# Row sums of attention: who reads the total out of its bank, and where the two rows are added

## The chip, the core and the metric

The kernel runs on one core of one Trainium2 chip. The core has TensorE (PE, matmuls; PEld is its weight load), VectorE (DVE), ScalarE (ACT), GpSimd (POOL) and SyncE (SP), whose queue issues the transfers. The engines run side by side, each in the order of its own instructions, and wait for each other on semaphores. The metric is the device time of one execution in microseconds; lower is better.

## What is computed

A decoder layer on 2048 tokens of width 1024: one input projection, causal attention with 8 heads on one side, a gated unit on the other, one output projection and a layer norm. The change touches the attention alone:

```
def one_block(args):
    qi, i = args
    sc = jnp.einsum('bqhd,bkhd->bhqk', qi, k).astype(jnp.float32) * scale
    ...
    sc = jnp.where(mask[None, None], sc, -jnp.inf)
    p = jax.nn.softmax(sc, axis=-1).astype(v.dtype)
    return jnp.einsum('bhqk,bkhd->bqhd', p, v)
```

The softmax divides by the sum of the exponentials of a query. The kernel sums them unnormalized and multiplies with the reciprocal at the end, together with the gate z_a.

## The kernel before

Three stages follow each other: projections and the gated unit (up to some 530 us), attention (to some 1010 us, with the first blocks of the output projection mixed in), and the rest of the output projection with the layer norm.

Attention works head by head (h = 0 to 7) and, in a head, by query tiles of 512 queries (qt = 0 to 3). Scores are laid out with keys on partitions and queries along the free axis. A unit is one block of 128 keys against one query tile: three matmuls of scores (L425 to L427, a high and a low part of each operand), the exponential on ACT in place in the bank (L435, `bank_a`), a high part by a cast on ACT (L441, `ph` or `xbuf`), the low part on DVE (L101, `pl`), and two matmuls with the values some four units later (L469 and L470, `bank_b`). POOL adds up the high parts over a tile's units (L454 and L456, `acc`), which is the larger part of the row sums. Meanwhile PE, DVE and ACT make the maxima of the next head's scores (L352 on PE into `bank_c`, L362 and L359 on DVE) and its keys and values. `bank_c` has two buffers, which these jobs and the total below share.

At the end of a tile, `finish_ops` folds the results. ACT copies half of one bank to `opair` (L527) and the whole other bank, which holds the low parts' sums and outputs, to `bsb` (L531); DVE and POOL add (L534, L537). For qt > 0, ACT casts `acc` to a high part (L555, `acch`), POOL makes the remainder (L101, `accl`), and PE multiplies both with ones (L564, `total`), so that every partition of a `bank_c` bank holds the total of the row sums. DVE adds one partition of this total to the row in `bsb` (L567, `row`), and SP gathers the row of 512 numbers onto 128 partitions by 4 (L581, `lc`). DVE takes the reciprocal there (L586), SP stores it to memory (L587, `r_d`), and for the odd head of a pair loads it back, spread over the partitions (L599, `rb`, two loads). POOL multiplies `opair` with the gate and with `rb` (L603), and SP stores the product (L609, `oa_d`). For qt = 0 there is no total and the row of `bsb` is gathered as it is.

The order on the engines is not that of the code. Every step is an `Op` with an engine, a cost from `LENGTH` (a fixed part and one per element), a rank and its dependences; `issue()` then picks, time step by time step in this model, the ready op of lowest rank, with buffers limited by `COUNT`. A different engine or cost for one op therefore moves other work on all engines. Each engine waits in its own order: an instruction that waits holds all behind it on that engine, transfers on SP's queue included. Loads of the last stage, such as those of `ln_g` into a buffer of `opair` (L1530), are placed on SP's queue among the last heads' transfers.

Of the kernel before, what the change touches and what calls it, by code (L numbers as in the profile page):

```python
# [15 lines left out]
ALU = mybir.AluOpType  # L16
# [40 lines left out]
def hybrid_layer_kernel(ctx: ExitStack, tc: tile.TileContext, xT, x, pos, w_feat, w_v, w_c,  # L57
# [3 lines left out]
    act, dve, pool, pe, sp = nc.scalar, nc.vector, nc.gpsimd, nc.tensor, nc.sync  # L61
# [35 lines left out]
    def f(ap):  # L97
        return ap.bitcast(F32)

    def sub(eng, out_, a, b):  # L100
        eng.tensor_tensor(out=out_, in0=a, in1=b, op=ALU.subtract)  # L101
# [7 lines left out]
    def bank_c():  # L109
        return ps_c.tile([P, 512], F32, name="bank_c")  # L110
# [40 lines left out]
    def raw2k(shape):  # L151
        return sb.tile(shape, F32, name="raw", tag="raw", bufs=5)
# [21 lines left out]
    def t2_tile(shape, dt, name, bufs):  # L174
        return pools["t2"].tile(shape, dt, name=name, tag=name, bufs=bufs)
# [94 lines left out]
    def op(eng, n, rank, fn, deps=(), times=1, takes=(), pair=None):  # L270
        fixed, per = LENGTH[eng]
        o = Op(eng, times * (fixed + per * n), rank, fn, deps, LAG[eng])
        o.takes += takes
        o.pair = eng == "pool" and n > 0 if pair is None else pair
        work.append(o)
        return o
# [128 lines left out]
    def tile_ops(h, qt, t_, q_, k_, e, g, own, oth):  # L405
# [5 lines left out]
        for n, j in enumerate(order):  # L411
# [99 lines left out]
            units.append(un)  # L511
            done["s"][h, qt] = s_
        finish_ops(h, qt, t_, e, own, oth, units[-1]["pv"], len(units) - 1)
        tiles.append(t_)

    pair = {}

    def finish_ops(h, qt, t_, e, own, oth, last, u):
        pr_ = h // 2
        ts = slice(qt * 512, (qt + 1) * 512)  # L520
        lr = slice(64 - 64 * e, 65 - 64 * e)

        def fold():
            if e == 0:
                pair[qt] = t2_tile([P, 512], F32, "opair", 4)
            t_["o"] = pair[qt]
            act.copy(out=t_["o"][own], in_=t_["a"][oth])  # L527

        def keep():
            t_["l"] = t2_tile([P, 512], F32, "bsb", 2)  # L530
            act.copy(out=t_["l"], in_=t_["b"])  # L531

        def add_a():
            dve.tensor_tensor(out=t_["o"][own], in0=t_["a"][own], in1=t_["o"][own], op=ALU.add)  # L534

        def add_b():
            pool.tensor_tensor(out=t_["o"][own], in0=t_["o"][own], in1=t_["l"][own], op=ALU.add)  # L537

        r = u + SKEW - 0.4
        f1 = op("act", 512, r, fold, [last])  # L540
        if e == 0:
            t_["o_freed"] = []
            f1.takes.append(("opair", t_["o_freed"]))
        else:
            t_["o_freed"] = tiles[-NT]["o_freed"]
        f2 = op("act", 512, r, keep, [last])
        f3 = op("dve", 512, r, add_a, [f1])
        f4 = op("pool", 512, r, add_b, [f2, f3])
        t_["out"] = [f2, f3]

        rows = [f2]
        if qt > 0:
            def cast():
                t_["ah"] = t2_tile([P, 512], F32R, "acch", 1)
                act.copy(out=t_["ah"], in_=t_["acc"])  # L555

            def rest():
                t_["al"] = t2_tile([P, 512], F32R, "accl", 1)
                sub(pool, t_["al"], t_["acc"], f(t_["ah"]))

            def total():
                t_["x"] = bank_c()
                for i, part in enumerate((t_["ah"], t_["al"])):
                    pe.matmul(t_["x"], ones, part, start=(i == 0), stop=(i == 1))  # L564

            def row():
                dve.tensor_tensor(out=t_["l"][lr], in0=t_["x"][lr], in1=t_["l"][lr], op=ALU.add)  # L567

            c_ = op("act", 512, r + 1, cast, [t_["adds"][-1]])
            s_ = op("pool", 512, r + 1.5, rest, [c_])  # L570
            m_ = op("pe", 512, r + 2, total, [s_], times=2)
            w_ = op("dve", 512, r + 2, row, [m_, f2])
            c_.takes.append(("acch", [m_]))
            s_.takes.append(("accl", [m_]))
            m_.takes.append(("c", [w_]))
            t_["freed"].append(s_)
            rows = [w_]

        def gather():
            t_["c"] = sb.tile([P, 2, 4], F32, name="lc", tag="lc", bufs=3)  # L580
            sp.dma_start(out=t_["c"][:, 0], in_=t_["l"][lr])  # L581

        r += 3
        g_ = op("sp", 0, r, gather, rows)
        f2.takes.append(("bsb", [g_, f4]))
        i_ = op("dve", 8, r, lambda: dve.reciprocal(t_["c"][:, 1], t_["c"][:, 0]), [g_])  # L586
        r_ = op("sp", 0, r, lambda: sp.dma_start(out=r_d[h, qt].rearrange("(p c) -> p c", c=4), in_=t_["c"][:, 1]), [i_])  # L587
        t_["r"] = r_
        if e == 1:
            mate = tiles[-NT]  # L590

            def load_z():
                t_["z"] = raw2k([P, 512])
                sp.dma_start(out=t_["z"], in_=za_d[pr_, :, ts])

            def load_r():
                t_["rb"] = t2_tile([P, 512], F32, "rb", 1)
                for i in range(2):
                    sp.dma_start(out=t_["rb"][64 * i:64 * i + 64],  # L599
                                 in_=r_d[h - 1 + i, qt:qt + 1, :].broadcast_to([64, 512]))  # L600

            def times(by):
                pool.tensor_tensor(out=t_["o"], in0=t_["o"], in1=t_[by], op=ALU.mult)  # L603

            z_ = op("sp", 0, r, load_z, [f3])
            b_ = op("sp", 0, r, load_r, [r_, mate["r"]], times=2)
            m1 = op("pool", 512, r, lambda: times("z"), [z_, f4])
            m2 = op("pool", 512, r, lambda: times("rb"), [b_, m1])
            o_ = op("sp", 0, r, lambda: sp.dma_start(out=oa_d[pr_, :, ts], in_=t_["o"]), [m2])  # L609
            z_.takes.append(("raw", [m1]))  # L610
            b_.takes.append(("rb", [m2]))
            t_["o_freed"].append(o_)
            done["oa"][pr_, qt] = o_
# [1033 lines left out]
```

## Time and profile before

| what | before |
|---|---|
| median of 3 runs | 1168.03 us (1166.73 to 1172.65) |
| profiled execution | 1166.87 us |
| its span, first to last instruction | 1165.1 us |
| PE busy | 1138.1 us (98%) |
| DVE busy | 840.6 us (72%) |
| ACT busy | 616.1 us (53%) |
| POOL busy | 498.4 us (43%) |
| mean granted clock | 0.997 |

Busy times are unions of the instructions' times over the whole span, so they average stages of different kind. Matmuls are pipelined and their ends are modelled: a PE that is called busy can still have small gaps. A wait is idle time in front of an instruction, put down to what came last; several waits for one instruction are not told apart. Idle time of an engine costs something only where another one then waits for it.

### The profile page before, as it was taken

The numbers are of one execution on the slowest core, as the hardware profiler recorded it, in microseconds if no ns is written. First come the engines' busy times: TensorE is split into PE (matmuls) and PEld (weight loads), VectorE is DVE, ScalarE is ACT, GpSimd is POOL, SyncE is SP. The second block draws the span as 40 slices with busy tenths as digits, with TensorE's granted clock in tenths as the row PEclk, the third lists the DMA queues.
The fourth block names the chain that finished last, engine by engine and source line by source line (L and its number), as shares of the span: only waits on it lengthen the run. The fifth ranks groups of instructions, "written<-read, shape, count | busy, mean of one in ns | idle before, by whom it ended". The sixth has DMA issues, their size and how long they took to land.

```text
span 1165.1 us, 17412 instructions
## 1 busy us (share of the span) xinstructions
PE 1138.1 (98%) x5497; PEld 937.5 (80%) x5497; DVE 840.6 (72%) x2022; ACT 616.1 (53%) x1203; POOL 498.4 (43%) x482
## 2 busy tenths in 40 slices
PE   7999999999999999999999999999999999999997
PEld 6888898878888898777878787777777877888886
DVE  4778476526762578648899989899899873339866
ACT  5552442337553424228888888887888883321000
POOL 1003201101112202116879998989799986400000
PEclk9999999999999999999999999999999999999999
DMA  7323672446145614541122212211227444676541
GB/s 253 98 74 98 175 219 97 145 159 196 57 169 170 199 47 143 165 128 59 29 64 65 64 35 60 72 46 37 65 59 204 154 125 125 182 241 214 191 136 64
DMA packets 87596, 142.27 MB, mean 122 GB/s; under 512 B 19584, under 2 KB 23696, under 8 KB 87312
## 3 DMA queue, kind: packets, MB, share of 16 engines
q1 hardware_dynamic: 87504, 141.16, 39.4%
q8 instruction: 43, 0.70, 0.3%
q14 instruction: 49, 0.40, 0.1%
HBM read 92.16 MB, written 48.82 MB: 121 GB/s over the span
## 4 chain that ended last, share of the span: by engine, by line
PE 84%; DVE 4%; POOL 4%; ACT 3%; DMA 2%; issue 2%; SPq 0%; DVEq 0%; POOLq 0%; ACTq 0%
PE bank_a L887 21%; PE bank_a L881 13%; PE bank_a L1415 11%; PE bank_c L352 5%; PE bank_b L469 4%; PE bank_a L425 4%; PE bank_b L470 4%; PE bank_a L426 4%; PE bank_a L427 4%; PE bank_c L1415 3%; POOL acc L456 2%; PE bank_a L1222 2%; PE bank_b L958 2%; DMA rb<-r_d 1%; PE bank_c L314 1%
## 5 line engine op out<-in xcount | busy, mean ns | idle before, releaser
L887 PE MATMUL bank_a<-xbuf,ring 128*128 128x512 f32 x1152 | 278.8, 394 | 6.5 <-ACT xbuf L712 6.1
L887 PEld LDWEIGHTS bank_a<-xbuf,ring 128*128 128x128 f32 x1152 | 216.0, 190 | 51.2 <-ACT xbuf L712 6.9
L456 POOL TENSOR_TENSOR acc<-acc,xbuf 128x512 f32<-128x512 f32 (+2 forms) x168 | 192.2, 1145 | 15.2 <-ACT xbuf L441 6.6
L435 ACT ACTIVATE bank_a<-bank_a 128x512 f32<-128x512 f32 (+1 forms) x288 | 163.6, 575 | 62.3 <-PE bank_a L427 39.8
L881 PE MATMUL bank_a<-ring,xbuf 128*128 128x512 f32 (+1 forms) x768 | 170.5, 373 | 0.0
L881 PEld LDWEIGHTS bank_a<-ring,xbuf 128*128 128x128 f32 x768 | 142.9, 189 | 17.0 <-DVE ring L101 0.2
L101 DVE TENSOR_TENSOR pl<-bank_a,xbuf 128x512 fp32r<-128x512 f32 (+1 forms) x192 | 126.1, 662 | 29.2 <-ACT xbuf L441 26.1
L362 DVE TENSOR_REDUCE mxt<-bank_c 128x1 f32<-128x512 f32 (+1 forms) x192 | 126.9, 667 | 19.0 <-PE bank_c L352 16.9
L470 PE MATMUL bank_b<-pl,xbuf 128*128 128x512 f32 (+1 forms) x320 | 116.9, 369 | 0.0
L441 ACT CAST xbuf<-bank_a 128x512 fp32r<-128x512 f32 (+1 forms) x192 | 107.7, 572 | 10.4 <-POOL acc L456 2.4
L101 DVE TENSOR_TENSOR ring<-raw,ring 128x512 fp32r<-128x512 f32 (+1 forms) x80 | 58.0, 739 | 51.2 <-ACT ring L712 46.5
L456 POOL TENSOR_TENSOR acc<-acc,ph 128x512 f32<-128x512 f32 (+1 forms) x72 | 83.9, 1165 | 5.3 <-ACT ph L441 1.1
L469 PE MATMUL bank_b<-xbuf 128*128 128x512 f32 (+2 forms) x216 | 80.6, 376 | 0.0
L101 DVE TENSOR_TENSOR pl<-bank_a,ph 128x512 fp32r<-128x512 f32 x96 | 65.1, 684 | 11.9 <-ACT ph L441 11.2
L359 DVE CUSTOM_DVE_ANT_0 bank_c<-bank_c,maskq 128x256 f32<-128x256 f32 (+3 forms) x128 | 65.8, 519 | 7.2 <-PE bank_c L352 6.0
L1000 ACT ACTIVATE act_t<-bank_a 128x512 f32<-128x512 f32 x40 | 23.9, 597 | 83.0 <-PE bank_a L887 82.8
L470 PEld LDWEIGHTS bank_b<-pl,xbuf 128*128 128x128 f32 x320 | 60.9, 190 | 8.3 <-DVE opair L534 0.3
L712 ACT CAST ring<-raw 128x512 fp32r<-128x512 f32 (+1 forms) x72 | 42.2, 600 | 45.7 <-PE bank_a L887 21.2
L425 PE MATMUL bank_a<-xbuf,ring 97*128 97x512 f32 (+2 forms) x160 | 61.8, 386 | 1.5 <-DVE pl L101 1.4
L101 POOL TENSOR_TENSOR held<-qrt 128x128 f32<-128x128 f32 x16 | 7.4, 461 | 128.2 <-DVE qrt L1180 98.2
L425 PE MATMUL bank_a<-q,ring 97*128 97x512 f32 (+2 forms) x160 | 60.8, 380 | 0.0
L352 PE MATMUL bank_c<-ring,xbuf 96*128 96x512 f32 (+2 forms) x160 | 59.9, 383 | 0.5 <-ACT mst L383 0.3
(219 smaller groups left out, 2341.1 us busy)
## 6 DMA issues: line engine op xcount, KB each, us to landing
raw<-in_w_feat_dram SPq DMA_DIRECT2D x48, 256.0 KB, 3.8
raw<-in_xT_dram SPq DMA_DIRECT2D x32, 256.0 KB, 4.0
out_dram<-pl SPq DMA_DIRECT2D x32, 256.0 KB, 2.1
xbuf<-ob_d SPq DMA_DIRECT2D x20, 256.0 KB, 6.5
raw<-in_w_out_dram SPq DMA_DIRECT2D x16, 256.0 KB, 4.2
wo_d<-wo_h SPq DMA_DIRECT2D x16, 256.0 KB, 2.0
wo_d<-raw SPq DMA_DIRECT2D x16, 256.0 KB, 3.1
ob_d<-act_h SPq DMA_DIRECT2D x16, 256.0 KB, 2.9
```

Of the source, the lines that this page charges most:

```text
L101: eng.tensor_tensor(out=out_, in0=a, in1=b, op=ALU.subtract)
L352: pe.matmul(st_["x"][:, :hi - lo], qs_(h, 0)[0:DQK, qb * P:end], kslot(h)[0:DQK, 0, lo:hi], start=True, stop=True)
L362: dve.tensor_reduce(out=mx[h][:, qb, c:c + 1], in_=xps, axis=AX.X, op=ALU.max)
L425: pe.matmul(o_, k_[0:DQK + 1, 0, js], q_[0][0:DQK + 1, qs], start=True, stop=False)
L435: act.activation(out=o_, in_=o_, func=AF.Exp, scale=SCALE)
L441: act.copy(out=un["ph"][:, c0:512], in_=un["x"][:, c0:512])
L456: pool.tensor_tensor(out=t_["acc"][:, cs], in0=t_["acc"][:, cs], in1=f(p_), op=ALU.add)
L469: pe.matmul(a_ps[:, cs], va, un["ph"][:, ps], start=first, stop=last)
L470: pe.matmul(b_ps[:, cs], vb, un["pl"][:, ps], start=first, stop=last and qt > 0)
L881: pe.matmul(dst[:, :n], a[:, k, js], b[:, 0:4, k, 0:cols], start=(k == 0 and i == 0), stop=(k == KT - 1 and i == 2))
L887: pe.matmul(dst, a[:, slot, k, :], b[:, k, :], start=(k == 0 and i == 0), stop=(k == KT - 1 and i == 2))
L1415: pe.matmul(y, mo(st, k, a)[:, js], wo(k, w)[:, ns], start=(k == kord(st)[0] and i == 0), stop=(k == kord(st)[-1] and i == 2))
```

## The change

The total is no longer added to the row in `bsb` by DVE. ACT copies it from its bank to another partition of the same `bsb` tile, 32 partitions on from the first row. SP gathers both rows, with two transfers, into the two halves of `lc`. There DVE adds them, 128 partitions by 4, and takes the reciprocal of the sum. The planner is told that the op `row` is ACT's now, that the gather costs two issues and that the reciprocal costs three.

```
-        lr = slice(64 - 64 * e, 65 - 64 * e)
+        lr, lr2 = slice(64 - 64 * e, 65 - 64 * e), slice(96 - 64 * e, 97 - 64 * e)
...
             def row():
-                dve.tensor_tensor(out=t_["l"][lr], in0=t_["x"][lr], in1=t_["l"][lr], op=ALU.add)
+                act.copy(out=t_["l"][lr2], in_=t_["x"][lr2])
...
-            w_ = op("dve", 512, r + 2, row, [m_, f2])
+            w_ = op("act", 512, r + 2, row, [m_, f2])
...
             sp.dma_start(out=t_["c"][:, 0], in_=t_["l"][lr])
+            if qt > 0:
+                sp.dma_start(out=t_["c"][:, 1], in_=t_["l"][lr2])
+
+        def invert():
+            c = t_["c"]
+            if qt > 0:
+                dve.tensor_tensor(out=c[:, 0], in0=c[:, 0], in1=c[:, 1], op=ALU.add)
+            dve.reciprocal(c[:, 1], c[:, 0])
...
-        g_ = op("sp", 0, r, gather, rows)
+        g_ = op("sp", 0, r, gather, rows, times=2 if qt else 1)
...
-        i_ = op("dve", 8, r, lambda: dve.reciprocal(t_["c"][:, 1], t_["c"][:, 0]), [g_])
+        i_ = op("dve", 8, r, invert, [g_], times=3 if qt else 1)
```

Lines behind this place have higher numbers in the changed kernel (L603 is L611, L1530 is L1538). What it moves is shown in three places. First, DVE at the first tile with a total (h = 0, qt = 1), before:

```order
L101 TENSOR_TENSOR pl<-bank_a,xbuf 128x512
L567 TENSOR_TENSOR bsb<-bank_c,bsb 1x512
L101 TENSOR_TENSOR pl<-bank_a,xbuf 128x384
L362 TENSOR_REDUCE mxt<-bank_c 128x1
L359 ISA bank_c,mxt<-bank_c,maskq 128x256
L359 ISA mxt 128x1
L101 TENSOR_TENSOR pl<-bank_a,ph_5123 128x512
```

and DVE at the same place in the changed kernel:

```order
L101 TENSOR_TENSOR pl<-bank_a,xbuf 128x512
L362 TENSOR_REDUCE mxt<-bank_c 128x1
L101 TENSOR_TENSOR pl<-bank_a,xbuf 128x384
L359 ISA bank_c,mxt<-bank_c,maskq 128x256
L359 ISA mxt 128x1
L101 TENSOR_TENSOR pl<-bank_a,ph_5123 128x512
L588 TENSOR_TENSOR lc<-lc 128x4
L589 RECIPROCAL lc<-lc 128x4
```

The addition to `bsb` is gone from between the low parts and the maxima, and a small addition stands in front of the reciprocal. On ACT a row `L567 COPY bsb<-bank_c 1x512` comes in between an exponential and a cast.

Second, POOL where the last product with `rb` of h = 1 (qt = 3) meets the remainder of h = 2, qt = 1, before:

```order
L454 TENSOR_TENSOR acc<-ph_5123,ph_5146 128x512
L603 TENSOR_TENSOR opair<-opair,rb 128x512
L456 TENSOR_TENSOR acc<-acc,xbuf 128x512
L537 TENSOR_TENSOR opair<-opair,bsb 64x512
L456 TENSOR_TENSOR acc<-acc,xbuf 128x512
L101 TENSOR_TENSOR accl<-acc,acch 128x512
```

and now:

```order
L454 TENSOR_TENSOR acc<-ph_5123,ph_5146 128x512
L101 TENSOR_TENSOR accl<-acc,acch 128x512
L611 TENSOR_TENSOR opair<-opair,rb 128x512
L456 TENSOR_TENSOR acc<-acc,xbuf 128x512
L537 TENSOR_TENSOR opair<-opair,bsb 64x512
```

The remainder `accl`, for which PE's total waits, has moved ahead of the product with `rb`.

Third, SP's queue in the last head (h = 7; `za_d` is the gate, `in_ln_g_dram` a weight of the last stage that goes into a buffer of `opair`), before:

```order
L581 DMA lc<-bsb 128x1x4
L609 DMA oa_d<-opair 128x512
L587 DMA r_d<-lc 128x4
L1439 DMA raw<-oa_d 128x512
L599 DMA rb<-r_d 64x512
L1530 DMA opair<-in_ln_g_dram 128x512
L599 DMA rb<-r_d 64x512
```

and now:

```order
L581 DMA lc<-bsb 128x1x4
L583 DMA lc<-bsb 128x1x4
L617 DMA oa_d<-opair 128x512
L1538 DMA opair<-in_ln_g_dram 128x512
L595 DMA r_d<-lc 128x4
L1447 DMA raw<-oa_d 128x512
L607 DMA rb<-r_d 64x512 x2
```

The load of `ln_g` has moved from between the two loads of `rb` to ahead of `r_d`, on which both depend.

## Rows read from the trace of the kernel before

**Rows 1.** The page's busy times: us (share of the span) xinstructions
```profile
PE 1138.1 (98%) x5497; PEld 937.5 (80%) x5497; DVE 840.6 (72%) x2022; ACT 616.1 (53%) x1203; POOL 498.4 (43%) x482
```
**Rows 2.** Stretches: start:end, length, busy (x) of PE, PEld, DVE, ACT, POOL; clock, DMA
```profile
600.00:660.00 60.00, 59.89 (x297) 47.52 (x296) 56.52 (x124) 50.61 (x96) 55.72 (x49) 1.00 0.27 72
...
1040.00:1100.00 60.00, 60.00 (x266) 49.71 (x265) 50.22 (x121) 8.09 (x18) 0.00 (x0) 1.00 0.67 218
```
**Rows 3.** The same columns, the whole attention stage
```profile
530.00:1010.00 480.00, 472.55 (x2313) 374.47 (x2312) 406.40 (x850) 381.50 (x735) 412.65 (x355) 1.00 0.29 82
```
**Rows 4.** Waits of PE's weight loads, 530 to 1010 us: total, times, longest us
```profile
PEld bank_c L564 <- POOL accl L101: 5.6, 6, 1.6
PEld bank_a L425 <- DVE pl L101: 4.0, 7, 1.2
PEld bank_c L352 <- DVE mxt L362: 3.8, 13, 0.5
PEld bank_c L352 <- DVE mxt L359: 3.4, 11, 0.5
```
**Rows 5.** Waits of ACT, 530 to 1010 us
```profile
ACT bank_a L435 <- PE bank_a L427: 39.8, 61, 2.7
```
**Rows 6.** The tile bsb: count, ns min/median/max, first and last start, forms
```profile
L531 ACT COPY bsb<-bank_b x32: 585/586/605, 534.1 to 1010.1; 128x512 f32<-128x512 f32 x32
L581 SPq DMA_DIRECT2D lc<-bsb x32: 476/516/556, 534.8 to 1017.1; - x32
...
L567 DVE TENSOR_TENSOR bsb<-bank_c,bsb x24: 668/684/689, 550.0 to 1011.5; 1x512 f32<-1x512 f32 x24
```
**Rows 7.** The tile lc: reciprocal, DVE's idle time before it, landing
```profile
L586 DVE RECIPROCAL lc<-lc x32: 154/168/180, 537.7 to 1019.1; 128x4 f32<-128x4 f32 x32
...
  DVE lc L586: 5.4, 5
...
DMA to landing us min/median/max: 1.4/2.0/2.4
```
**Rows 8.** Waits of POOL, 530 to 1010 us
```profile
POOL opair L603 <- DMA rb<-r_d: 8.9, 7, 3.3
```
**Rows 9.** POOL's timeline at 660 us: start, length us, instruction, idle time before
```profile
660.34 1.28 POOL L603 TENSOR_TENSOR opair<-opair,rb 128x512 f32<-128x512 f32 x1 [1.31 <-DMA rb<-r_d]
...
665.33 1.27 POOL L101 TENSOR_TENSOR accl<-acc,acch 128x512 fp32r<-128x512 f32 x1
```
**Rows 10.** SP's queue, 950 to 971 us, same columns
```profile
955.19 0.33 SPq L609 DMA_DIRECT2D oa_d<-opair  x1
956.75 0.33 SPq L587 DMA_DIRECT2D r_d<-lc  x1
...
957.95 0.45 SPq L599 DMA_DIRECT2D rb<-r_d  x1
958.44 1.82 SPq L1530 DMA_DIRECT2D opair<-in_ln_g_dram  x1
960.31 0.45 SPq L599 DMA_DIRECT2D rb<-r_d  x1
```
**Rows 11.** POOL's timeline behind it
```profile
964.64 1.29 POOL L603 TENSOR_TENSOR opair<-opair,rb 128x512 f32<-128x512 f32 x1 [3.27 <-DMA rb<-r_d]
...
976.35 1.26 POOL L101 TENSOR_TENSOR accl<-acc,acch 128x512 fp32r<-128x512 f32 x1
```
**Rows 12.** PE's timeline there
```profile
975.87 0.51 PE L564 MATMUL bank_c<-acch,zo 128*128 128x512 f32 x1 [0.96 <-ACT acch L555]
977.67 0.51 PE L564 MATMUL bank_c<-accl,zo 128*128 128x512 f32 x1 [1.30 <-POOL accl L101]
```
**Rows 13.** The stretch behind the stall, columns as in rows 2
```profile
978.00:980.00 2.00, 2.00 (x6) 1.60 (x5) 1.49 (x3) 0.52 (x1) 0.86 (x1) 0.52 0.59 163
```

## The prediction

> **What bounds the kernel now.** I read the page's busy shares first, then the attention stage by stretches, then the waits of PE's weight loads, then the rows of the tile finish that the change touches, and last two timelines. The page shows PE busy for 98% of the span at full granted clock, DVE 72%, ACT 53%, POOL 43% [rows 1]. That is a mean over stages. The change touches only the attention stage, from 530 us to 1010 us, where all four engines are loaded: PE 472.6, DVE 406.4, ACT 381.5 and POOL 412.7 us of 480 [rows 3]. In a full stretch, 600 to 660 us, DVE has 56.5 and POOL 55.7 us of 60 [rows 2]. So PE is the bound, DVE and POOL are close behind it, and ACT has room: 98.5 us idle in the stage, of which 39.8 us is the exponential waiting for PE's scores [rows 5].
>
> How much is there to win? In the output stage, 1040 to 1100 us, PE never waits, and its weight loads fill 49.7 of 60 us, 83% [rows 2]. In the attention stage they fill 374.5 of 480 us, 78% [rows 3]. If the mix of tiles were the same, the gap of 5% would be about 24 us: an estimate of all that any change of waits could give here. The waits that have a name are smaller: PE's loads wait 5.6 us in 6 places for POOL's remainder of the row sums (accl), and 4.0 + 3.8 + 3.4 = 11.2 us in 31 places for DVE (pl, and the two kinds of maximum) [rows 4].
>
> [...] Read bare, the 78% would leave 22% to win; the stage in which PE never waits shows that this share tops out near 83% here, so I don't follow the bare reading in the sum. It comes back as a rival.
>
> **The change part by part.** The sum starts from the profiled execution: 1166.87 us, of which 1165.1 is its span; the median of the runs, 1168.03, lies 1.16 above it. Of 32 tile finishes, 24 have a second row sum (the four query tiles of eight heads, less the first of each).
>
> *A. The row leaves DVE.* Removed: 24 x 0.684 us = 16.4 us [rows 6]. Added: 24 additions of 128 x 4; no row shows one, the nearest is the reciprocal of the same shape, 0.168 us [rows 7], so 4.0 us. DVE gets 12.4 us of 406.4 back, 3%. It is worth between nothing (if none of the rows stood ahead of something PE waited for) and 11.2 us (if every wait for DVE went). The 31 waits are 0.36 us each; a row stands in DVE's queue once per 20 us, a wait comes once per 15 us, and I take it that a quarter of the waits have a row just ahead of them: 8 x 0.36 = 2.9 us. Some of that returns, because DVE's reciprocal, now behind a second transfer, waits longer: today it waits 5.4 us in 5 of 32 cases [rows 7]. I take **-2.0 us**.
>
> *B. ACT copies it.* A copy of one partition by 512 out of a bank is not in the trace; the copy of 128 x 512 from such a bank takes 0.586 us [rows 6]. So 24 x 0.586 = 14.1 us on ACT, which goes from 381.5 to 395.6 of 480. What hides it is ACT's idle time in front of the exponential, 39.8 us [rows 5]. Behind the copy on ACT stand the next exponentials and casts, and for them wait DVE's pl and then PE. Without that cover it is 14.1 us; with it, nothing. A gain is excluded, since no ACT work is removed. The copy's wait for PE's total is short for the same reason as DVE's was. ACT keeps 84 of its 98 us of idle time, so I take **+0.5 us**.
>
> *C. The chain of the sums gets longer.* Per tile: the copy for the row, 0.586 - 0.684 = -0.1; a second gather on SP's queue, 0.516 us of issue [rows 6]; the addition, 0.17. Together +0.59 us. The first gather doesn't start earlier, since both wait for the copy. At the end of this chain POOL waits, in order, with its sums for the next tile queued behind: it sits 8.9 us in 7 of the 16 products with rb [rows 8]. Seven times 0.59 is 4.1 us, all sixteen 9.4 us. PE pays only where it then waits for accl (5.6 us in all [rows 4]). Here the new order matters. The planner has moved the work of some twelve tiles by one to four units. At 660.34 us POOL waited 1.31 us for rb with the next accl four instructions behind [rows 9]; now accl stands ahead of that product, and PE's wait for it should go. In others the product comes earlier against its chain. Bounds are -5.6 (all six waits go) and +4.1 (each longer chain reaches PE). I take **-0.5 us**, the two nearly cancelling.
>
> *D. One place on SP's queue near the end.* Before, the queue stood, for the tile h = 7, qt = 1: store oa_d of the tile ahead 955.19, r_d 956.75, first rb 957.95, a load of ln_g into a buffer of opair (1.82 us on the queue), second rb 960.31 [rows 10]. The product with rb started at 964.64 after 3.27 us of idle, from there POOL worked without a gap up to accl at 976.35 [rows 11], and PE stood idle for 0.96 us before the first matmul of the total and 1.30 us before the second, 2.3 us [rows 12]. Now the load of ln_g stands in front of r_d, and both rb come behind. It takes its buffer from a store of opair, at the latest the one issued just ahead of it. Its 1.82 us may be that wait or its own length, since the other issues of this stretch take 0.33 to 0.45 us [rows 10]. If the store is through by 957.5 and the load takes 0.33 us, r_d leaves at 957.9, the first rb 1.2 us behind it (as 957.95 - 956.75) and the last rb at 959.6, 0.7 us earlier than before. If the load ends at 960.3 as before, r_d leaves then, and the last rb at 962.0 to 962.8, up to 2.5 us later (1.2 us behind r_d as here, or 2.0 as these small transfers land in the median [rows 7]). POOL has no gap in which to take a delay up before accl, and PE is full from there to the end. Between -0.7 and +2.5 us I take **+1.2 us**, nearer the late end, because a store that frees the buffer is right ahead in either case. [...]
>
> Sum: -2.0 + 0.5 - 0.5 + 1.2 = -0.8 us. 1166.87 - 0.8 + 1.16 = **1167.2 us** as a median: no change that can be told.
>
> **The rivals.**
> *Faster: DVE was what held PE.* If 60% of DVE's waits go (-6.7), the POOL waits mostly go with the new order (-4.0) and D goes the early way (-0.7): 1168.0 - 11.4 = 1156.6. For it: DVE at 94% in full stretches [rows 2]. Against: only 3% of DVE's work goes, and most of PE's lost time has no DVE name. Chance 0.11.
>
> [...] If PE is far from its limit, as 78% of weight loads suggests, the stage would follow DVE's work: -12.4 us, 1155.6. The trace speaks against it (83% is full here). Chance 0.03. [...]
>
> *Slower: POOL's queue.* All sixteen products wait 0.59 us longer, 9.4 us of POOL time, half of which reaches PE through accl (+4.7), D costs 2.5 and one more stall brings the lower clock (+1.6): 1168.0 + 8.8 = 1176.8. It decides once POOL's idle time in front of rb is over some 13 us (8.9 + 4.1), since POOL has under 5 us of slack in a stretch of 60 [rows 2]. Chance 0.16. [...] The row shows 2.0 us to landing for 2 KB [rows 7]. If the second gather paid that in full rather than its issue alone, the chain would grow by 2.1 us, and this rival would be the forecast; the two are on one queue and can run together, so I don't expect it.
>
> *It doesn't do what it says.* DVE's freed time goes into waiting for the second gather: 24 x 0.59 = 14.2 us, more than the 12.4 won. Then A is nil and the time is 1167.2 + 2.0 = 1169.2, still no change. Chance 0.17.
>
> **How the numbers follow.** A measurement of this kernel tells some 0.5%, 5.8 us, from no change: under 1162.2 is faster, over 1173.9 slower. Forecast 0.53 and the last rival 0.17 are both "same": 0.70. Faster 0.14, slower 0.16. The range leaves out about 0.09 below and 0.1 above: 1161.5 to 1174.5.
>
> **What would show it.** DVE's row of 0.684 us is gone and 24 additions near 0.17 us are there; 24 copies on ACT near 0.59 us; DVE's busy time in the stage falls by 12 us and ACT's rises by 14 us (A, B). PE's waits for DVE fall from 11.2 to about 9 us (A). POOL's idle time before rb rises from 8.9 to 11 to 13 us (C). Near 960 us r_d leaves behind ln_g, and PE's stall at L564 grows from 2.3 to some 3.5 us (D). I am wrong if DVE's waits fall by half, if the copy takes far from 0.59 us, or if stalls of over 1 us show up in new places.

## The result, and the profile after

The changed kernel takes **1179.19 us** (median of 6 runs, 1178.63 to 1181.38) where the kernel before, run beside it, takes 1168.78 (6 runs, 1166.73 to 1172.65): a ratio of **1.0092, 95% interval 1.0075 to 1.0109**, so 10.4 us slower. The forecast was 1167.2 with a range up to 1174.5. The profiled execution took 1179.39 us, its span is 1177.7. Lines behind the change stand 8 further down in the code (L603 is L611, L586 is L589); L588 is the new addition.

Busy times of the page, as in [rows 1], and the attention stage as in [rows 3], here up to 1022 us, since the stage ends some 12 us later now:

```profile
PE 1145.7 (97%) x5497; PEld 941.3 (80%) x5497; DVE 838.2 (71%) x2022; ACT 628.3 (53%) x1227; POOL 499.5 (42%) x482
```

```profile
530.00:1022.00 492.00, 478.88 (x2319) 377.33 (x2319) 404.04 (x851) 393.41 (x760) 413.37 (x355) 0.99 0.28 80
```

DVE should have lost 12 us over the program and lost 2.4 (840.6 to 838.2). Where the rest stayed is in the rows of the tiles lc and bsb (count, ns min/median/max, first and last start, forms):

```profile
L588 DVE TENSOR_TENSOR lc<-lc x24: 152/659/1244, 554.7 to 1032.1; 128x4 f32<-128x4 f32 x24
L589 DVE RECIPROCAL lc<-lc x32: 163/178/179, 540.0 to 1032.3; 128x4 f32<-128x4 f32 x32
...
L531 ACT COPY bsb<-bank_b x32: 558/587/592, 536.4 to 1022.7; 128x512 f32<-128x512 f32 x32
...
L567 ACT COPY bsb<-bank_c x24: 577/578/585, 551.4 to 1024.2; 1x512 f32<-1x512 f32 x24
```

The copies cost what was forecast. The additions do not: 0.659 us in the median where the reciprocal of the same shape takes 0.178, and they spread from 0.15 to 1.24. The groups by line show them with their sum (busy us, mean ns, idle time before):

```profile
L588 DVE TENSOR_TENSOR lc<-lc 128x4 f32<-128x4 f32 x24 | 15.2, 631 | 6.1 <-DMA lc<-bsb 5.6 <-issue 0.3
```

15.2 us for 24 x 4 elements a partition, nearly the 16.4 us of the row that went. The timeline of one of them (start, length us), first DVE, then the instruction that GpSimd runs meanwhile, then the weight load of PE that waits:

```profile
671.04 1.24 DVE L588 TENSOR_TENSOR lc<-lc 128x4 f32<-128x4 f32 x1
672.32 0.18 DVE L589 RECIPROCAL lc<-lc 128x4 f32<-128x4 f32 x1
672.41 0.66 DVE L362 TENSOR_REDUCE mxt<-bank_c 128x1 f32<-128x512 f32 x1
...
670.98 1.28 POOL L456 TENSOR_TENSOR acc<-acc,xbuf 128x512 f32<-128x512 f32 x1
...
673.13 0.19 PEld L352 LDWEIGHTS bank_c<-ring,xbuf 96*128 96x128 f32 x1 [0.53 <-DVE mxt L362]
...
674.33 0.19 PEld L352 LDWEIGHTS bank_c<-ring,xbuf 96*128 96x128 f32 x1 [0.78 <-DVE mxt L362]
...
714.13 0.16 DVE L588 TENSOR_TENSOR lc<-lc 128x4 f32<-128x4 f32 x1
```

The addition starts at 671.04, just after a POOL instruction (670.98), and ends at 672.28, 0.02 us after that instruction (672.26). Behind it in DVE's queue stand the reciprocal and then a maximum (mxt) of the next head's scores, and two of PE's weight loads wait for this maximum and the next one, 0.53 and 0.78 us. At 714.13 POOL is idle and the addition takes 0.16 us. I went through all 24: 21 end 0.01 to 0.03 us after the POOL instruction that they fell on, two found POOL idle (161 and 164 ns), one fell on an instruction's last 0.06 us (152 ns). So an addition doesn't work for 0.66 us, it is held until GpSimd's instruction is over, and DVE's queue with it.

What PE's weight loads wait for, 530 to 1022 us, as in [rows 4], and POOL's wait before rb, as in [rows 8]:

```profile
PEld bank_c L352 <- DVE mxt L362: 7.4, 16, 1.0
PEld bank_c L352 <- DVE mxt L359: 5.3, 17, 0.5
PEld bank_c L379 <- DVE mrow L375: 5.0, 8, 1.5
PEld bank_c L564 <- POOL accl L101: 3.6, 3, 1.8
PEld bank_c L564 <- ACT acch L555: 2.3, 1, 2.3
PEld bank_a L425 <- DVE pl L101: 1.5, 5, 0.4
...
POOL opair L611 <- DMA rb<-r_d: 16.6, 10, 3.8
```

The row for mrow (made from the maxima) in the kernel before, which [rows 4] leaves out:

```profile
PEld bank_c L379 <- DVE mrow L375: 1.0, 4, 0.4
```

The waits for the maxima grew from 7.2 to 12.7 us, those for mrow from 1.0 in 4 places to 5.0 in 8. All groups of this view whose releaser is DVE's pl, mxt or mrow, the small ones included, sum to 13.5 us in the kernel before and 22.6 here: **+9.1 us**. That sum is the measure used below. It is not time lost one for one, since PE's matmuls still run while the next weight load waits (at 788.76 us the load has waited 0.98 us, PE 0.56). By PE's own busy time its idle time in the stage grew from 7.5 us (480 less 472.55 [rows 3]) to 13.1 us (492 less 478.88), by 5.7. Near the end of the stage something else is added: PE's timeline at the last total (idle time in brackets), then two stretches with the columns of [rows 2], and the same places in the kernel before:

```profile
987.25 0.50 PE L564 MATMUL bank_c<-acch,zo 128*128 128x512 f32 x1 [1.88 <-ACT acch L555]
989.05 0.79 PE L564 MATMUL bank_c<-accl,zo 128*128 128x512 f32 x1 [1.30 <-POOL accl L101]
```

```profile
988.00:995.00 7.00, 5.95 (x14) 4.70 (x15) 3.15 (x5) 3.21 (x6) 2.23 (x2) 0.53 0.38 125
790.00:794.00 4.00, 3.59 (x10) 2.70 (x10) 3.96 (x11) 1.49 (x4) 2.72 (x3) 0.57 0.02 1
```

```profile
978.00:985.00 7.00, 7.00 (x25) 5.56 (x24) 2.87 (x5) 3.12 (x6) 1.50 (x2) 0.76 0.48 150
790.00:794.00 4.00, 4.00 (x21) 3.17 (x20) 3.97 (x9) 3.22 (x7) 3.48 (x4) 1.00 0.29 91
```

The stall of [rows 12] grew from 2.26 to 3.18 us, and behind it the granted clock is at its lower level for most of 7 us (0.50 from 989 to 995, mean 0.53 over the stretch shown; in the kernel before 0.76 over 978 to 985, which makes 3.4 us at half speed against 6.6 here). A second such stretch is new at 790 us, behind three pauses of PE of 0.36 to 0.56 us; there the mean of 4 us was 1.00 before. PE's wait for accl fell from 5.6 to 3.6 us.

Not every difference between the two profiled executions belongs to the change. Over 520 to 532 us, ahead of the first changed instruction, the mean granted clock is 0.57 in the changed kernel and 1.00 in the kernel before, behind nearly the same pause of PE (1.08 and 1.09 us), and the first copy of bsb starts 2.3 us later (536.4 against 534.1 [rows 6]). From the first to the last of these copies the stage takes 476.0 us before and 486.3 now, 10.3 more.

### The profile page after: what moved, and what is told of

Its sections match the earlier page's. It is cut to its first block, busy times and chain, and to the rows that moved or that the text cites. A ratio compares the mean times of both kernels' runs of the same rounds, so it can differ in the third digit from the quotient of the medians.

```text
span 1177.7 us, 17488 instructions
## 1 busy us (share of the span) xinstructions
PE 1145.7 (97%) x5497; PEld 941.3 (80%) x5497; DVE 838.2 (71%) x2022; ACT 628.3 (53%) x1227; POOL 499.5 (42%) x482
## 4 chain that ended last, share of the span: by engine, by line
PE 76%; DVE 8%; ACT 5%; DMA 4%; POOL 3%; issue 3%; SPq 0%; DVEq 0%; POOLq 0%; ACTq 0%
PE bank_a L895 20%; PE bank_a L889 13%; PE bank_a L1423 11%; PE bank_c L352 4%; PE bank_a L425 4%; PE bank_b L469 4%; PE bank_a L426 3%; PE bank_a L427 3%; PE bank_b L470 3%; PE bank_c L1423 3%; POOL acc L456 2%; DVE pl L101 2%; PE bank_b L966 1%; PE bank_a L1230 1%; DVE mxt L362 1%
## 5 line engine op out<-in xcount | busy, mean ns | idle before, releaser
L101 DVE TENSOR_TENSOR pl<-bank_a,ph 128x512 fp32r<-128x512 f32 x96 | 65.5, 685 | 13.7 <-ACT ph L441 12.9
L352 PE MATMUL bank_c<-ring,q 96*128 96x512 f32 (+2 forms) x160 | 59.6, 391 | 2.8 <-DVE mxt L362 0.9
```

Of the source, the lines that this page charges most:

```text
L352: pe.matmul(st_["x"][:, :hi - lo], qs_(h, 0)[0:DQK, qb * P:end], kslot(h)[0:DQK, 0, lo:hi], start=True, stop=True)
```

## The experiments

Theories. **PORT**: the addition is held by GpSimd's instructions, and what it holds behind it is the price. **ORDER**: the planner's new order costs. **CHAIN**: the second gather makes rb later. Others are named where they are expected. Each ratio is against the kernel before, run beside it on the same chip, with its 95% interval. The expectations that give microseconds start from 1168.8 us for the kernel before; beside e1 to e4 it took 1172.6, so they are read here as ratios. The changed kernel was not run again beside these kernels, so a comparison with it is one of two ratios. "Waits for DVE" is the sum described above, in one profiled execution of each kernel.

### Order and instructions apart

*e1_reduce.* The changed kernel, with the addition as a reduction, which has one input:

```
...
-    dve.tensor_tensor(out=c[:, 0], in0=c[:, 0], in1=c[:, 1], op=ALU.add)
+    dve.tensor_reduce(out=c[:, 2], in_=c[:, 0:2].rearrange("p a b -> p b a"), axis=AX.X, op=ALU.add)
...
```

> The changed kernel with its order on every engine kept; only DVE's addition of the two gathered rows is made as a reduction over a 128 x 4 x 2 view, which has one input tensor in place of two (the small tile gets a third slot and two buffers in place of three). Theory PORT (the addition with two inputs in on-chip memory waits until POOL's running instruction ends: 0.66 us in the median where 0.17 was forecast): the reduction takes some 0.16 us, DVE gets 24 x 0.5 = 12 us back, and the time falls from 1179.2 by more than half of the loss, to 1168 to 1173. Theory ORDER (the planner's new order is what costs): the reduction is fast as well, but the time stays at 1176 to 1180. Theory CHAIN (the second gather and the longer way to the reciprocal hold up POOL in front of rb): 1176 to 1180, POOL's idle time before rb stays near 16 us.

*e2_order_only.* The changed kernel's order (its planner entries stay), with the instructions of before:

```
-    act.copy(out=t_["l"][lr2], in_=t_["x"][lr2])
+    dve.tensor_tensor(out=t_["l"][lr], in0=t_["x"][lr], in1=t_["l"][lr], op=ALU.add)
```

and neither second gather nor addition. The order is the changed kernel's on PE, DVE, ACT and POOL; on SP's queue the load of ln_g comes behind rb here.

> The order of the changed kernel with the instructions of the kernel before: the planner is told the new engine and costs, but DVE adds the total to the row out of its bank, one gather, no small addition. PORT: 1167 to 1171, near the kernel before. ORDER: 1176 to 1180, near the changed kernel. CHAIN: 1167 to 1171.

*e3_instr_only.* The reverse: the change's instructions with the planner entries of before (row as "dve", no times=2 and times=3). The load of ln_g stands between the two loads of rb, as before.

> The order of the kernel before with the instructions of the change: the planner is told the old engine and costs, but ACT copies the total, both rows are gathered and DVE adds them (two inputs). PORT: 1175 to 1181, with additions of 0.66 us in the median. ORDER: 1166 to 1170. CHAIN: 1174 to 1180, POOL's idle time before rb near 16 us.

*e4_instr_reduce.* e3 with the reduction of e1.

> As the run before (old order, ACT copies, two gathers), with the reduction of one input in place of the addition. PORT: 1164 to 1169, not slower than the kernel before. ORDER: 1164 to 1170. CHAIN: 1174 to 1180.

Measured: e1 **1.0031** (1.0010 to 1.0051), e2 **1.0000** (0.9981 to 1.0019), e3 **1.0080** (1.0054 to 1.0106), e4 **1.0000** (0.9982 to 1.0019). The tile lc in e1, then the same instruction in e3 and e4, as groups:

```profile
L588 DVE TENSOR_REDUCE lc<-lc 128x4 f32<-128x8 f32 x24 | 3.7, 154 | 5.0 <-DMA lc<-bsb 4.7
```

```profile
L588 DVE TENSOR_TENSOR lc<-lc 128x4 f32<-128x4 f32 x24 | 13.7, 570 | 7.6 <-DMA lc<-bsb 7.6
```

```profile
L588 DVE TENSOR_REDUCE lc<-lc 128x4 f32<-128x8 f32 x24 | 3.7, 155 | 8.2 <-DMA lc<-bsb 7.9 <-issue 0.3
```

ORDER falls: the new order with the old instructions costs nothing (e2), and the old order with the new instructions costs about what the whole change does (e3). PORT stands: the same sum over the same numbers with one input takes 0.155 us on average (0.142 to 0.165), and takes 0.61% (e1) or 0.80% (e3 to e4) off. CHAIN falls as the main cause: e4 has the whole longer chain, POOL waits 15.4 us before rb in it, and its time is that of before. One detail of PORT missed: the additions in e3 took 0.507 us in the median, not 0.66. And e1's median of 1176.0 us lies in PORT's range (1168 to 1173) only as a ratio, beside a kernel before of 1172.6.

A lower granted clock is a rival that none of these theories names. The 27 runs of the kernel before beside e1 to e4 go from 1167.0 us at a mean granted clock of 0.999 to 1175.6 at 0.990; a straight line through them gives some 0.8 us for each 0.001, an estimate from these runs. e3's six runs have 0.991 on average against 0.992, which by that estimate makes 1 us of its 9.6. So the clock isn't what the additions cost. It is more of the small remainders: e1's runs have 0.990 against 0.992, some 2 us of its 3.5. Whether its own stalls lowered the clock there isn't shown.

### Is it the wait itself, or having something there?

Three kernels put one useless instruction before each of the 24 reciprocals of the kernel before: two inputs (x3), one input and short (x4), one input and as long as the waits (x5). x1 has the row's move to ScalarE alone.

*x1_copy_alone* (one gather, of the total's row; the low parts' share of the sums is left out):

```
-    dve.tensor_tensor(out=t_["l"][lr], in0=t_["x"][lr], in1=t_["l"][lr], op=ALU.add)
+    act.copy(out=t_["l"][lr2], in_=t_["x"][lr2])
...
-    sp.dma_start(out=t_["c"][:, 0], in_=t_["l"][lr])
+    sp.dma_start(out=t_["c"][:, 0], in_=t_["l"][lr2 if qt > 0 else lr])
```

> Old order; ACT copies the total to a second row, and the one gather takes that row alone, without the addition: the sums of the low parts are left out of the row sums. So DVE loses its 24 rows of 0.684 us, ACT has 24 copies of 0.58 us, and neither a second gather nor an addition is there. Theory PORT: as fast as the reduction in the old order or faster, 0.994 to 1.000 of the kernel before. Theory CHAIN (the second gather eats what DVE's relief brings): clearly faster than the reduction in the old order, 0.990 to 0.995 of before. Rival ACT (the copy on ACT costs as much as DVE's relief brings): 0.998 to 1.004.

*x3_dummy_two*, *x4_dummy_one*, *x5_dummy_long* (in these three the load of ln_g has moved ahead of r_d, as in the changed kernel):

```
+    dve.tensor_tensor(out=c[:, 1], in0=c[:, 0], in1=c[:, 0], op=ALU.add)                        # x3
+    dve.tensor_reduce(out=c[:, 1], in_=c[:, 0:1].rearrange("p a b -> p b a"), axis=AX.X, op=ALU.add)  # x4
+    dve.tensor_reduce(out=c[:, 1, 0:1], in_=maskq, axis=AX.X, op=ALU.max)                       # x5
```

> The kernel before with one useless instruction more in front of each of the 24 reciprocals: a DVE addition of 128 x 4 with two inputs in on-chip memory, whose result is overwritten. The row stays on DVE, one gather, nothing new on ACT. PORT: it waits for POOL's running instruction, 0.5 to 0.7 us in the median, and the time is 1.005 to 1.010 of before. Rival WORK (any instruction in this place costs, whatever its inputs): the same as the next run. Rival JOINT (the wait alone is harmless, it costs only together with the copy and the second gather): 1.000 to 1.003.

> As the run before, the useless instruction being a reduction with one input (128 x 4 x 1). PORT: 0.15 us each, 24 x 0.15 = 3.6 us on DVE, 0.999 to 1.003 of before. WORK: as the run before.

> As the run before, the useless instruction being a long reduction with one input, 128 x 512 of a constant, some 0.6 us: as long as the addition's wait, but without a second input. If the price of the wait is the time that DVE is held up, whatever holds it: 1.004 to 1.010 of before, as with the two inputs. If the price lies in how the two engines hold each other up: 1.000 to 1.004, below the run with two inputs.

Measured: x1 **1.0021** (1.0003 to 1.0039), x3 **1.0064** (1.0037 to 1.0091), x4 **1.0037** (1.0018 to 1.0056), x5 **1.0091** (1.0055 to 1.0126). The useless instruction in x3, x4 and x5 in turn:

```profile
L589 DVE TENSOR_TENSOR lc<-lc 128x4 f32<-128x4 f32 x24 | 11.6, 485 | 5.2 <-DMA lc<-bsb 5.0
```

```profile
L589 DVE TENSOR_REDUCE lc<-lc 128x4 f32<-128x4 f32 x24 | 3.6, 150 | 5.5 <-DMA lc<-bsb 5.3
```

```profile
L589 DVE TENSOR_REDUCE lc<-maskq 128x1 f32<-128x512 bf16 x24 | 16.2, 674 | 0.1
```

x5's instruction is never held (662 to 686 ns each) and costs as much as the whole change. So DVE's time at this place has a price whatever fills it, and being held by GpSimd is one way to fill it. x3, whose addition took 0.463 us in the median, doesn't settle it alone: its distance from x4 is 0.27%, and the two intervals overlap; x4 lies just above the range that PORT gave it (0.999 to 1.003). The parting of a held instruction from a short one rests on e3 to e4 and on the changed kernel to e1, that of a long one from a short one on x5 to x4. x5 has four runs (1176.2 to 1182.7 us). x1 missed PORT's range (0.994 to 1.000) and lies in that of ACT: taking the row off DVE and giving it to ScalarE gains nothing.

### One part out, one part alone, and the plan

*a1_no_add.* The changed kernel without its addition:

```
...
-    dve.tensor_tensor(out=c[:, 0], in0=c[:, 0], in1=c[:, 1], op=ALU.add)
-    dve.reciprocal(c[:, 1], c[:, 0])
+    dve.reciprocal(c[:, 1], c[:, 1 if qt else 0])
```

> The changed kernel with its 24 additions taken out and nothing else: copy, both gathers, and the order on every engine stay. (Left out: the low parts' share of the total, so the outputs lack it.) PORT (the two-input addition waits for GpSimd and holds VectorE; that is the most part of the 0.9%): 1.000 to 1.004 of before, 6 to 10 us under the changed kernel; the wait of GpSimd before rb falls from 16.6 us to 9 to 12. REST (the addition is a small part, the copy on ScalarE and the second gather in the changed order cost most): 1.005 to 1.009. With the reduce kernel in the same order at 1.0031, the difference of this one to it is the price of 24 short one-input instructions: under 0.2% if they are short wherever they fall, 0.3% or more if any instruction put there costs.

*x2_gather_alone.* The kernel before with a second gather of the same row:

```
+    if qt > 0:
+        sp.dma_start(out=t_["c"][:, 1], in_=t_["l"][lr])
```

> The kernel before with a second, useless gather of the same row in each of the 24 tiles (into the other half of lc, which the reciprocal then writes over); row on VectorE, no copy, no addition. CHAIN (0.5 to 0.6 us more on SP's queue between row and reciprocal makes rb later and GpSimd waits): GpSimd's wait before rb 11 to 13 us instead of 8.9, time 1.002 to 1.004. Not CHAIN: wait up by under 1.5 us in all or hidden, time 0.998 to 1.002. PORT says nothing of this one beyond no price for VectorE: VectorE's busy time as before within 1 us.

*p1_planner_told.* The changed kernel, planned with the mark that other two-input work of DVE has:

```
-    i_ = op("dve", 8, r, invert, [g_], times=3 if qt else 1)
+    i_ = op("dve", 8, r, invert, [g_], times=3 if qt else 1, pair=True)
```

> The changed kernel with the planner told that the addition and reciprocal exclude a GpSimd instruction (the same mark that it has on other two-input VectorE work); the instructions are the same, their order changes. PORT holds in any order as long as the plan's times are not the chip's: GpSimd is busy 85 to 89% of this stretch, so the additions stay near 0.5 to 0.7 us each and the time at 1.006 to 1.011. PLAN (the plan can put the additions into GpSimd's gaps): additions under 0.3 us median and the time at 1.000 to 1.004.

Measured: a1 **1.0018** (1.0004 to 1.0033), x2 **1.0024** (1.0006 to 1.0041), p1 **1.0043** (1.0024 to 1.0061). Taking out 24 additions takes 0.74% off, some 8.7 us, so the addition is the most part of the loss; order, copy, second gather and the missing row on DVE together leave 0.2%. x2's wait before rb came out higher than either side had put it, and its time in CHAIN's range:

```profile
POOL opair L605 <- DMA rb<-r_d: 14.4, 8, 3.6
```

p1 went between the two forecasts. The additions are held less, but are held (median 0.398 us):

```profile
L588 DVE TENSOR_TENSOR lc<-lc x24: 152/398/1272, 554.7 to 1021.8; 128x4 f32<-128x4 f32 x24
```

The mark halves the loss in this plan; since its order differs from the changed kernel's in many places (POOL's wait before rb is 18.8 us, the highest of all), that the mark alone did it isn't shown.

### The relief of DVE without ScalarE

*z1_row_gone.*

```
-    dve.tensor_tensor(out=t_["l"][lr], in0=t_["x"][lr], in1=t_["l"][lr], op=ALU.add)
+    dve.tensor_tensor(out=t_["l"][lr, 0:4], in0=t_["x"][lr, 0:4], in1=t_["l"][lr, 0:4], op=ALU.add)
...
-    dve.reciprocal(t_["c"][:, 1], t_["c"][:, 0])
+    dve.tensor_scalar(out=t_["c"][:, 1], in0=t_["c"][:, 0], scalar1=2.0, scalar2=None, op0=ALU.max) if qt else dve.reciprocal(t_["c"][:, 1], t_["c"][:, 0])
```

> The kernel before with VectorE's row cut from 512 to 4 elements in 24 tiles, nothing put on ScalarE, one gather, no addition; the reciprocal of those tiles becomes a maximum with a constant of the same shape. (Left out: the total's share of the row sums.) The order on TensorE, GpSimd and ScalarE is that of before; only the load of ln_g moves ahead of r_d. RELIEF (VectorE's 16.4 us are worth time, and in the changed kernel the copy on ScalarE eats it): some 12 us of VectorE's time go, TensorE's waits for VectorE fall from 13.5 to 8 to 11 us, time 0.990 to 0.996. PLACE (a row stands where nobody waits behind it, so its removal is worth nothing, copy or not): waits for VectorE 12 to 15 us, time 0.998 to 1.002. The moved load alone may cost up to 0.2% in either case.

Measured: **1.0023** (1.0007 to 1.0038), on neither side. The rows say why (the tiles bsb and lc):

```profile
L567 DVE TENSOR_TENSOR bsb<-bank_c,bsb x24: 139/154/160, 550.0 to 1017.5; 1x4 f32<-1x4 f32 x24
...
L586 DVE TENSOR_SCALAR lc<-lc x24: 158/510/1268, 553.1 to 1024.7; 128x4 f32<-128x4 f32 x24
L586 DVE RECIPROCAL lc<-lc x8: 161/164/173, 537.7 to 948.0; 128x4 f32<-128x4 f32 x8
```

The maximum, chosen as a stand-in for the reciprocal, takes as long, and as unevenly, as the additions that GpSimd held (0.158 to 1.268 us, 0.510 in the median), though it has one input; the reciprocals of the other eight tiles take 0.161 to 0.173. So the kernel took 12 us off DVE and put 13.5 us of standing on it, where the 24 reciprocals had taken 4, and the question that it was made for isn't settled. It has one use: beside x3 it has no row and no copy, and is 0.41% faster (0.10 to 0.72, from the two intervals). That hints at the row being worth something as long as ScalarE doesn't get it, but z1 also has less standing at this place (13.5 us against 11.6 and some 4 for the reciprocals behind it), and the two ran on different chips. It is one comparison of two kernels that differ in more than one instruction.

### All of them beside each other

| kernel | held or added on DVE, us each | waits for DVE, us | POOL before rb, us | ratio |
|---|---|---|---|---|
| before | none | 13.5 | 8.9 | 1 |
| e2, order only | none | 14.5 | 10.7 | 1.0000 |
| a1, no addition | none | 15.2 | 9.7 | 1.0018 |
| x1, copy alone | none | 13.7 | 13.3 | 1.0021 |
| x2, gather alone | none | 16.1 | 14.4 | 1.0024 |
| e1, reduction | 0.154 | 15.7 | 10.5 | 1.0031 |
| e4, reduction, old order | 0.155 | 17.2 | 15.4 | 1.0000 |
| x4, short | 0.150 | 16.7 | 14.5 | 1.0037 |
| z1, row gone | 0.563 | 17.3 | 14.1 | 1.0023 |
| p1, planner told | 0.537 | 20.0 | 18.8 | 1.0043 |
| x3, two inputs | 0.485 | 20.5 | 16.5 | 1.0064 |
| x5, long | 0.674 | 21.9 | 13.7 | 1.0091 |
| after | 0.631 | 22.6 | 16.6 | 1.0092 |
| e3, old order | 0.570 | 23.1 | 15.9 | 1.0080 |

By and large the time follows PE's waits for DVE, and these follow how long DVE stands at this place. It doesn't follow POOL's wait before rb: 15.4 us with no loss in e4, 13.7 with the full loss in x5. The ratios are of medians, the other columns of one execution that can lie apart from them: x5's took 1176.2 us where its median is 1181.5, e1's 1170.1 where it is 1176.0. Below 0.4% the ratios don't add up (x1, x2 and x4 each cost 0.2 to 0.4% alone, e4 has the parts of all three and costs nothing), and the granted clocks of the runs differ by as much, so I don't split that remainder among copy, gather and order. No kernel here is faster than the one before; e2 and e4 equal it.

## Why the prediction was wrong

**A, the addition: the step that failed.** I priced 24 additions by the reciprocal, 0.168 us [rows 7], 4.0 us in all, and wrote that no row shows one. They took 0.631 on average, 15.2 us, so DVE got 1.2 us back and not 12.4, and with the wait in the queue the term A, bounded by nothing and a gain of 11.2 us, was a loss. The mistake was to look for the nearest row only in the tile finish and to price it by its median. By its kind (two inputs, both in SBUF) rows of the kernel before had shown the wait, L1059 in the very shape, here against rows with a bank for one input:

```profile
L101 DVE TENSOR_TENSOR pl<-bank_a,ph x96: 655/684/693, 532.1 to 1003.4; 128x512 fp32r<-128x512 f32 x96
L101 DVE TENSOR_TENSOR xbuf<-raw,xbuf x40: 673/691/1773, 6.0 to 1046.0; 128x512 fp32r<-128x512 f32 x40
...
L1059 DVE TENSOR_TENSOR csm<-cmv x8: 143/164/339, 163.4 to 446.0; 128x4 f32<-128x4 f32 x8
...
L929 DVE TENSOR_SCALAR sm<-mv x8: 160/169/1262, 32.9 to 323.8; 128x2 f32<-128x2 f32 x8
```

From a bank and SBUF: 96 instances within 38 ns. From SBUF and SBUF: the same median and a longest of 1773. L1059 has the shape of the new addition, 128 x 4 with two inputs in SBUF: median 164, longest 339, and three of its eight end 0.02 us behind an instruction of GpSimd. A small instruction with one input of two elements (L929): median 169, longest 1262, which ends 0.03 us behind one. The maximum, not the median, carries the news, and how often it strikes depends on GpSimd: 43% busy over the span [rows 1], but 412.7 of 480 us in this stage [rows 3]. An addition that finds an instruction of 1.28 us with 86% chance, anywhere in it, is held 0.55 us on average, plus its own 0.15: an estimate of 0.7, against 0.631 measured, that needed nothing but [rows 3] and the length of a product in [rows 9]. The kernel's planner treats such work so: other two-input work of DVE is marked there as excluding GpSimd (pair=True); the row, with a bank for one input, has no mark (its 24 took 0.668 to 0.689 us [rows 6]), and the addition got none.

**A, the relief.** Taken as -2.0 us. DVE's waits rose instead, and where the additions are out or cheap (a1, e1, e4) the whole of the rest is worth nothing or costs 0.2 to 0.3%. Whether a quarter of the waits had a row just ahead of them, these runs don't tell: z1 beside x3 hints at a relief, and x1 shows none once the copy stands on ScalarE. DVE's busy time hardly changed in sum (-2.4 us); what changed is where it stands. The same time at the row's place brought nothing when it went (x1), and cost 0.9% ahead of the reciprocal (x5).

**B** was right in the copy's price (0.578 us against 0.586); that its cover is whole isn't shown, since copy and relief were only seen together.

**C.** Forecast: POOL's wait before rb 11 to 13 us, -0.5 us of time. It is 16.6 us, because the reciprocal now also stands behind a held addition: in the same order it is 9.7 without the addition (a1) and 10.5 with a short one (e1). The decision point of the rival "POOL's queue" (13 us) was passed, and its 1176.8 us lies nearest to the result, but its mechanism is not what happened: e4 passes that point too and loses nothing, and PE's wait for accl fell, as C said. A rival that gives about the right number isn't shown by it. No run shows the 1.6 us that its sum has for the lower clock behind one more stall; the new stretch at 790 us stands behind three pauses of 0.36 to 0.56 us, and its 3.4 us at half speed make some 1.7 us by estimate.

**D.** The stall grew by 0.9 us (forecast +1.2). The reason given is there: r_d leaves right behind the load of ln_g,

```profile
968.22 0.34 SPq L1538 DMA_DIRECT2D opair<-in_ln_g_dram  x1
968.62 0.42 SPq L595 DMA_DIRECT2D r_d<-lc  x1
```

1.1 us after the reciprocal ends at 967.54. Before, it left 0.03 us after the reciprocal (956.72 to 956.75 [rows 10]). But it isn't the only one: e4 and x1 issue r_d ahead of that load, and their first wait at the total is 1.47 and 1.79 us all the same, against 0.96 before and 1.88 after. What the place added beyond the sum is the clock: the stretch at the lower level behind the stall is 6.6 us and not 3.4, 3.2 us more at half speed, 1.6 us. That the longer stall made it longer isn't shown: in a1 the stall is longer still (2.29 and 1.31 us) and the stretch is 3.4 us.

**"It doesn't do what it says"** came nearest as a mechanism, though not in its time of 1169.2 us: DVE's freed time is used up by waiting, only not for the second gather but for GpSimd.

**Sum of what the profile shows.** The stage is 10.3 us longer in the two profiled executions. Waits of the weight loads: +9.1 (for DVE), +0.9 (D's stall), -2.0 (accl); lower clock at 790 and 988 us, 3.4 + 3.2 us more at half speed: +3.3. That makes 11.3 us, too much, since not all of a weight load's wait is lost. By PE's own idle time, +5.7 for the waits of every kind, it makes 9.0. So the waits are the larger part and the lower clock about a third. The stretch at 790 us may be chance: e2 has one at the same place (0.72 over 790 to 796 us) and its time is that of the kernel before.

## What to carry to other kernels

Price a new DVE instruction by where its operands lie before its size: look up the longest, not the median, of rows of the same kind in stretches where GpSimd is busy; if the longest is the median plus the most part of a GpSimd instruction, expect to be held by GpSimd's busy share times half of its instruction. As an estimate this is on the high side: with the instruction's own time it gives 0.7 us here, where the five kernels with a held instruction have means of 0.485 to 0.631. A tiny sum of two SBUF rows was better written as a reduction over both (0.142 to 0.165 us in e1 and e4). And 16 us taken off an engine that is 85% busy gained nothing that could be measured, where the next engine of the same chain had to take it.

## What was new about the chip

A 128 x 4 TENSOR_SCALAR with one fp32 input in SBUF took up to 1.27 us (median 0.510 in z1), while RECIPROCAL and TENSOR_REDUCE of that size stayed at 0.163 to 0.179 (changed kernel) and 0.133 to 0.160 (x4). The hold of an addition ends 0.01 to 0.03 us after GpSimd's instruction (21 of 24 in the changed kernel), that of a TENSOR_SCALAR of 128 x 2 in the kernel before 0.03 us after it (L929, 1.262 us). What holds DVE there, and why RECIPROCAL with its one input isn't held like TENSOR_SCALAR, is left unexplained by these runs. And the stretch of the lower clock behind a stall isn't set by the stall's length alone: 3.4 us behind idle times of 0.96 and 1.30 us (before) and behind 2.29 and 1.31 (a1), 6.6 us behind 1.88 and 1.30 (after).
